# One core of a Trainium2: keys and values of two token blocks turned by VectorE in 32x32 squares and a DRAM round trip in place of TensorE transposes

## The chip, the cores and the metric

The kernel runs on one core of one Trainium2 chip. The metric is the device time of one execution in microseconds (us). Three runs of the kernel before took 2595.07, 2595.23 and 2595.78 us, median 2595.23 us. The profile was taken on one more execution of the same program.

## What is computed

One step of an encoder layer: a wide projection of the normed input, a short convolution (path A), a gated linear attention with a state (path B), three output projections, norms and a gate. All of it is in float32. The change lies in path B, which works on 8 heads of 128 channels in chunks of 64 tokens:

```python
def hgrn2_block(S, q, k, v, logf):
    L = q.shape[1]
    b = jnp.cumsum(logf, axis=1)
    ref = b[:, (L - 1) // 2][:, None]
    qe = q * jnp.exp(b - ref)
    ke = k * jnp.exp(ref - b)
    att = jnp.where(causal, jnp.einsum('bthk,bshk->bhts', qe, ke), 0.0)
    o = jnp.einsum('bhts,bshv->bthv', att, v) + jnp.einsum('bthk,bhkv->bthv', q * jnp.exp(b), S)
    b_last = b[:, -1]
    S_new = jnp.exp(b_last)[..., None] * S + jnp.einsum('bshk,bshv->bhkv', k * jnp.exp(b_last[:, None] - b), v)
    return S_new, o
```

The sum over tokens s in the state update and in `att` times `v` needs keys and values with the tokens on the partitions. The projections give them with the channels on the partitions, so each 128x128 tile of them has to be turned.

## The kernel before

**Blocks.** The 2112 tokens (2048 of a prompt, 64 of a sample) are worked in three blocks of 768, 704 and 640 tokens. Two chunks of 64 tokens make a pair, a full 128x128 tile. A block has 6, 5 and 5 pairs; the second block has the sample's 64 tokens besides. `plan()` puts them into parts: the first four pairs, the other pairs, and the sample alone (called single in the code).

**Products.** Nearly all TensorE time goes into the projections. Two 128-wide output blocks are made together by seven products over half operands (`sgroup`), and each product is 12 matmuls: 4 blocks of the contraction, each as three matmuls of a rounded high part and a rest (lines 444 to 446). The weights' parts come by DMA, which SP asks for: 256 KB each, a raw block and its rest.

**Heads.** For each head `path_b` calls `head_prep`, which runs two such groups: forget gate and query, then output gate and value, 14 products in all. VectorE and ScalarE make the decayed keys `kb` and `ka`, the queries `qe` and `qx`, the values `vt` and the gate `z`. `scaled` (it makes `kb`, lines 993 to 1003, and then `qx`, line 1013) is called after the third product of the second group; `vt` (lines 1022 and 1023) is ready about when that group ends.

**Hooks.** The attention of a head doesn't run at once. `path_b` puts its steps into the list `hooks`, and after each product of the next head `sgroup` takes one entry from it. A step's matmuls are thus queued on TensorE right behind that product (`placed`). In the second and third block a part has four steps (`head_attn`):

- step 0: TensorE transposes of `kb` (line 1068) and `vt` (line 1070), ScalarE copies of both from PSUM to SBUF (lines 1072 and 1073), the products of keys and queries (lines 1083 and 1084) and their masking on VectorE (line 1092);
- step 1: the state updates, one matmul for each pair (line 1098), then a chain of VectorE operations from pair to pair (line 1115);
- step 2: the outputs (lines 1138 and 1140) and their norm, for which POOL computes a power (line 691);
- step 3: the transposes back (line 1156) and the product with the gate (line 1158).

With two or three parts, step 0 of the parts stands behind products 0, 1, 2 of the next head, step 1 behind 3, 4, 5, step 2 behind 6, 7, 8 and step 3 behind 10, 11, 12. At the end POOL stores the head's result to DRAM (line 1166).

**Queues.** Every engine works its own instructions in the compiled order. SP asks for the weights; POOL asks for nearly everything else that moves. A POOL DMA that needs what an earlier one wrote waits in POOL's queue until that one has landed, and all that is behind it on POOL waits too.

**Buffers.** Wide tiles come from one ring of 48. PSUM has 5 banks for products and 3 for the attention.

Of the kernel before, what the change touches and what calls it, by code (L numbers as in the profile page):

```python
# [18 lines left out]
P = 128  # L19
# [74 lines left out]
def hybrid_step(  # L94
# [66 lines left out]
    def ps_attn():  # L161
        return psa.tile([P, 512], F32, tag="pa", name=nm("pa"))
# [773 lines left out]
    def head_prep(bl, hc, hd, first, hs):  # L936
        n, npair = bl["n"], bl["npair"]
        nch, np1 = n // CH, npair * P
        sf, qe = rt(), rt()
        sq = None if first else rt()  # L940

        def sink_f(c, h, x, y):
            if c == 0:
                A.activation(half(sf, h), whole(x, y), AF.Sigmoid)
            else:
                into(half(qe, h), x, y)

        if hs and hd == 0:
            plain_group(FF * 8, QQ * 8, hs, sink_f)
        else:  # L950
            sgroup(FF * 8 + hd, QQ * 8 + hd, hc, sink_f, first)
        if not first:
            A.activation(sq, qe, AF.Sigmoid)
        lg, b, eq = rt(), rt(), rt()
        A.activation(lg, sf, AF.Ln, bias=lb[:, hd : hd + 1], scale=omlb[:, hd : hd + 1])
        if not first:
            V.scalar_tensor_tensor(qe, qe, QK_SCALE, sq, ALU.mult, ALU.mult)
            V.tensor_scalar(sf, sf, nomlb[:, hd : hd + 1], omlb[:, hd : hd + 1], ALU.mult, ALU.add)
        V.tensor_tensor_scan(b, keep[:, :n], lg, 0.0, ALU.mult, ALU.add)
        ref = chunks(b)[:, :, CH // 2 - 1 : CH // 2]  # L960
        V.tensor_tensor(chunks(lg), chunks(b), ref.to_broadcast([P, nch, CH]), ALU.subtract)
        qc = small.tile([P, 2, BN // CH], F32, tag="qc", name=nm("qc"))
        f, r = qc[:, 0, :nch], qc[:, 1, :nch]
        ka, kb, qx, vt, z = hf(npair * CH), rt(), rt(), rt(), rt()

        late = first and hd > 0

        def scaled(after):


            with tc.issue_after(after):
# [12 lines left out]

            ka3 = ka.rearrange("p (g t) -> p g t", t=CH)
            more = npair - 2 * SWAP
            for lo, hi, to in (
                (0, SWAP, ka3[:, more + 1 :: 2, :]),
                (SWAP, 2 * SWAP, ka3[:, more : npair - 1 : 2, :]),
                (2 * SWAP, npair, ka3[:, :more, :]),  # L990
            ):
                own = slice(2 * lo, 2 * hi, 2)
                V.tensor_tensor(to, chunks(sf)[:, own, :], chunks(lg)[:, own, :], ALU.mult)
                scale = f2[:, lo:hi].unsqueeze(2).to_broadcast([P, hi - lo, CH])
                place = slice(2 * lo + (hi <= SWAP), 2 * hi, 2)
                V.tensor_tensor(chunks(kb)[:, place, :], to, scale, ALU.mult)
            for lo, hi in ((0, SWAP), (SWAP, npair)):
                seconds, place = slice(2 * lo + 1, 2 * hi, 2), slice(2 * lo + (hi > SWAP), 2 * hi, 2)
                V.tensor_tensor(chunks(kb)[:, place, :], chunks(sf)[:, seconds, :], chunks(lg)[:, seconds, :], ALU.mult)
            if nch % 2:  # L1000
                end = slice(nch - 1, nch)
                V.tensor_tensor(chunks(kb)[:, end, :], chunks(sf)[:, end, :], chunks(lg)[:, end, :], ALU.mult)
            V.tensor_tensor(f2, f2, f1, ALU.mult)
            if not late:
                queries()

        def queries():
            if first:
                A.activation(qe, qe, AF.Silu)
                V.scalar_tensor_tensor(qe, qe, QK_SCALE, eq, ALU.mult, ALU.mult)  # L1010
            else:
                V.tensor_tensor(qe, qe, eq, ALU.mult)
            V.tensor_tensor(chunks(qx), chunks(qe), f.unsqueeze(2).to_broadcast([P, nch, CH]), ALU.mult)

        def sink_v(c, h, x, y):
            if c == 1:
                n1 = 0
                if h == 0:
                    n1 = 2 * SWAP * CH
                    for odd in range(2):  # L1020
                        c3, to = (slice(o, 2 * SWAP, 2) for o in (odd, 1 - odd))
                        V.tensor_tensor(chunks(vt)[:, to, :], chunks(x[:, :n1])[:, c3, :], chunks(y[:, :n1])[:, c3, :], ALU.add)
                V.tensor_tensor(half(vt, h)[:, n1:], x[:, n1:], y[:, n1:], ALU.add)
# [12 lines left out]
        return dict(eq=eq, f=f, ka=ka, kb=kb, qe=qe, qx=qx, vt=vt, z=z, more=npair - 2 * SWAP, first=first, last=bl["last"], carry=None)  # L1036

    def cols3(t, nt):
        return t[:, : nt * P].rearrange("p (g c) -> p g c", c=P)

    def head_attn(ip, gs, d, hd):

# [19 lines left out]

        p_k, p_v = ps_attn(), ps_attn()
        with placed():
            for i, g in enumerate(gs):
                T.transpose(p_k[:, i * P : i * P + P], cols(d["kb"], g), ident)
            for i, g in enumerate(gs):
                T.transpose(p_v[:, i * P : i * P + P], cols(d["vt"], g), ident)  # L1070
        kt, v = tile3(0), tile3(1)
        A.copy(kt[rows], cols3(p_k, nt)[rows])
        A.copy(v[rows], cols3(p_v, nt)[rows])
        p_a = ps_attn()
        with placed():
            for i, g in enumerate(gs):
# [18 lines left out]
        p_u = ps_attn()  # L1095
        with placed():
            for i in range(nt):
                T.matmul(p_u[:, i * P : i * P + P], kt[:, i, :], v[:, i, :], start=True, stop=True)  # L1098
        ss = tile3()
        prevs = []  # L1100
        sample = gs[0]["sample"]
# [33 lines left out]
        with placed():  # L1135
            for i, g in enumerate(gs):
                dst = p_o[:, i * P : i * P + P]
                T.matmul(dst, att[:, i, :], v[:, i, :], start=True, stop=prevs[i] is None)  # L1138
# [19 lines left out]
        V.scalar_tensor_tensor(z[:, c], p_t[:, P - ln : P - ln + n], g_on[:, hd : hd + 1], z[:, c], ALU.mult, ALU.mult)  # L1158
        yield

    def path_b(bl, hc, first, kept, fills, hs, lead_sums=None):


# [4 lines left out]
        for hd in range(NH):  # L1168
            d = head_prep(bl, hc, hd, first, hs)
            if hd > 0 if first else hd == KH + 1:  # L1170
                next(fills, None)
            assert not hooks
            lead = first and hd == 0
            attn = [head_attn(i, gs, d, hd) for i, gs in enumerate(bl["parts"])]
            hooks.extend([None] * (2 * lead))
            for step in range(4):
# [3 lines left out]
                if lead_sums is not None and not first and step == 2:  # L1180
                    hooks[-1] = partial(next, lead_sums, None)
# [530 lines left out]
```

## Time and profile before

| | |
|---|---|
| three timed runs | 2595.07, 2595.23, 2595.78 us |
| profiled execution, first to last instruction (span) | 2590.9 us |
| TensorE busy (weight loads) | 2572.4 us (2556.1 us) |
| VectorE, ScalarE, POOL busy | 1726.9, 1530.4, 368.3 us |
| granted TensorE clock | 1.000 |
| moved by DMA | 739.87 MB, mean 286 GB/s |

For the profiled execution only the span was recorded. The median of the timed runs is 4.3 us above it: what lies around the span. The heads of the second block run from about 1083 to 1399 us of the span, those of the third from about 1900 to 2180 us.

In a row of the timeline stand the start (us), the busy time (us), the engine, the line, the operation, what is written and read, the shape, and how many were merged (x4). PEld is the load of a matmul's stationary operand. In brackets stands the idle time before it and who ended that.

### The profile page before, as it was taken

Reading aid. Unit: us, or ns where it says so; the run is one execution under the profiler, and the core shown is the slowest. Engines: PE = TensorE matmul, PEld = TensorE weight load, DVE = VectorE, ACT = ScalarE, POOL = GpSimd, SP = SyncE. Lnnn points to the kernel's source line nnn. Section 1 sums busy time; section 2 is a strip of 40 time slices with the busy share of each in tenths; the row PEclk is TensorE's granted clock in tenths of the full one; section 3 lists DMA queues with packets and bytes.
Section 4 is the critical chain, followed back from the end, with each engine's and each line's share of the span. In section 5 each row is a group of like instructions: output and inputs, shape, how many; then the busy total and the mean of one; then the engine's idle time right before and its main releaser. Section 6 shows DMA issues by size and latency. Waiting matters only on the chain.

```text
span 2590.9 us, 47524 instructions
## 1 busy us (share of the span) xinstructions
PE 2572.4 (99%) x16436; PEld 2556.1 (99%) x16436; DVE 1726.9 (67%) x3500; ACT 1530.4 (59%) x2973; POOL 368.3 (14%) x677
## 2 busy tenths in 40 slices
PE   9999999999999999999999999999999999999999
PEld 9999999999999999999999999999999999999998
DVE  7788778888777775466464556987345545336967
ACT  6766676455453764466564555566456665446675
POOL 2011111230022021111111221102100000001011
PEclk9999999999999999999999999999999999999999
DMA  8678777899897888877768998989887788999986
GB/s 325 224 262 288 263 260 273 310 360 308 262 349 238 272 311 269 281 248 233 262 227 287 342 388 313 323 291 334 295 268 251 246 273 264 299 297 323 333 270 200
DMA packets 361234, 739.87 MB, mean 286 GB/s; under 512 B 44119, under 2 KB 48785, under 8 KB 360993
## 3 DMA queue, kind: packets, MB, share of 16 engines
q1 hardware_dynamic: 321696, 582.69, 67.3%
q0 software_dynamic: 39296, 154.14, 16.3%
q8 instruction: 129, 2.11, 0.3%
q14 instruction: 113, 0.92, 0.1%
HBM read 543.44 MB, written 193.22 MB: 284 GB/s over the span
## 4 chain that ended last, share of the span: by engine, by line
PE 90%; DMA 4%; DVE 4%; issue 1%; ACT 1%; SPq 0%; POOL 0%; DVEq 0%; ACTq 0%
PE pg L444 19%; PE pg L446 19%; PE pg L445 19%; PE pg L596 5%; PE pg L595 5%; PE pg L597 5%; PE pg L635 3%; PE pg L634 3%; PE pg L633 3%; PE pa L1098 1%; PE pa L1138 1%; DMA lo<-low 1%; PE pa L1140 1%; PE pa L1084 1%; DMA low<-lo 1%
## 5 line engine op out<-in xcount | busy, mean ns | idle before, releaser
L444 PE MATMUL pg<-r,hi 128*128 128x320 f32 (+2 forms) x3304 | 1086.4, 329 | 1.4 <-DVE r L492 0.7
L445 PE MATMUL pg<-r,hi 128*128 128x320 f32 (+2 forms) x3304 | 1067.6, 323 | 0.0
L446 PE MATMUL pg<-r,lo 128*128 128x384 f32 (+2 forms) x2356 | 768.8, 326 | 5.3 <-DMA lo<-low 3.4
L275 ACT CAST hi<-raw 128x512 fp32r<-128x512 f32 x730 | 449.7, 620 | 515.5 <-PE pg L445 179.2
L444 PEld LDWEIGHTS pg<-r,hi 128*128 128x128 f32 x3304 | 621.5, 188 | 3.3 <-issue 1.0
L445 PEld LDWEIGHTS pg<-r,hi 128*128 128x128 f32 x3304 | 621.9, 188 | 0.0
L446 PEld LDWEIGHTS pg<-r,lo 128*128 128x128 f32 x2356 | 442.5, 188 | 7.9 <-DMA lo<-low 4.4
L446 PE MATMUL pg<-r,s 128*128 128x352 f32 (+1 forms) x948 | 299.4, 316 | 0.3 <-DMA s<-low 0.3
L596 PE MATMUL pg<-r,hi 128*128 128x320 f32 (+2 forms) x864 | 277.4, 322 | 0.6 <-DVE r L228 0.6
L595 PE MATMUL pg<-r,hi 128*128 128x320 f32 (+2 forms) x864 | 275.0, 322 | 0.0
L228 ACT CAST hi<-raw 128x512 fp32r<-128x512 f32 x252 | 155.6, 620 | 155.5 <-PE pg L445 44.0
L228 DVE TENSOR_TENSOR r<-r,r 128x320 fp32r<-128x320 f32 (+7 forms) x354 | 208.7, 608 | 52.9 <-ACT r L228 51.3
L228 ACT CAST r<-r 128x320 fp32r<-128x320 f32 (+7 forms) x354 | 185.9, 557 | 57.0 <-DMA r<-w_blk 13.0
L228 DVE TENSOR_TENSOR lo<-raw,hi 128x512 fp32r<-128x512 f32 x231 | 157.9, 685 | 88.0 <-ACT hi L228 84.2
L597 PE MATMUL pg<-r,lo 128*128 128x352 f32 (+2 forms) x564 | 180.9, 321 | 0.7 <-DMA lo<-low 0.7
L446 PEld LDWEIGHTS pg<-r,s 128*128 128x128 f32 x948 | 177.9, 188 | 0.7 <-DMA s<-low 0.6
L228 ACT CAST hi<-s 128x512 fp32r<-128x512 f32 x156 | 96.2, 618 | 120.1 <-PE pg L445 102.0
L634 PE MATMUL pg<-r,hi 128*128 128x384 f32 (+2 forms) x512 | 166.8, 326 | 0.2 <-DVE r L228 0.2
L633 PE MATMUL pg<-r,hi 128*128 128x384 f32 (+2 forms) x512 | 166.3, 328 | 0.2 <-ACT hi L275 0.2
L596 PEld LDWEIGHTS pg<-r,hi 128*128 128x128 f32 x864 | 162.2, 188 | 2.4 <-DVE r L228 1.7
L595 PEld LDWEIGHTS pg<-r,hi 128*128 128x128 f32 x864 | 161.3, 188 | 1.3 <-ACT r L228 0.6
L458 ACT COPY hf<-pg 128x352 f32<-128x352 f32 (+2 forms) x354 | 157.1, 446 | 1.7 <-PE pg L446 1.3
(403 smaller groups left out, 4114.3 us busy)
## 6 DMA issues: line engine op xcount, KB each, us to landing
raw<-w_blk SPq DMA_DIRECT2D x577, 256.0 KB, 4.1
raw<-S SPq DMA_DIRECT2D x444, 256.0 KB, 4.2
lo<-low SPq DMA_DIRECT2D x422, 256.0 KB, 4.1
s<-low SPq DMA_DIRECT2D x308, 256.0 KB, 4.0
low<-lo SPq DMA_DIRECT2D x271, 256.0 KB, 3.8
S<-s SPq DMA_DIRECT2D x152, 256.0 KB, 3.6
low<-r POOLq DMA_DIRECT2D x54, 256.0 KB, 5.1
r<-w_blk POOLq DMA_DIRECT2D x52, 256.0 KB, 6.9
```

The lines of the kernel that those rows point to most:

```text
L228: return A.copy(hi, src).ins, V.tensor_tensor(lo, src, hi.bitcast(F32), ALU.subtract).ins
L275: A.copy(hi, raw)
L444: add(hi[:, k, :], xhi, start=start and k == 0, stop=False)
L445: add(hi[:, k, :], xlo, start=False, stop=False)
L446: last[0] = add(lo[:, k, :], xhi, start=False, stop=k == KH - 1).ins
L458: copied = A.copy(got[n], ps[bank])
L595: add(hi[:, k, :], xhi, start=start and k == 0, stop=False)
L596: add(hi[:, k, :], xlo, start=False, stop=False)
L597: last[0] = add(lo[:, k, :], xhi, start=False, stop=k == KH - 1).ins
L633: T.matmul(ps, hi[:, k % 4, :], xhi[:, c], start=k == ks[0], stop=False)
L634: T.matmul(ps, hi[:, k % 4, :], xlo[:, c], start=False, stop=False)
L635: last[0] = T.matmul(ps, lo[:, k % 4, :], xhi[:, c], start=False, stop=k == ks[-1]).ins
```

## The change

Only the second and third block are touched (`first` is false), and there only the pairs; the sample's single part keeps its TensorE transposes.

- `turned` is new. For `kb` at the end of `scaled`, and for `vt` after the second group, one VectorE instruction transposes all 32x32 squares of the 5 pairs at once: a square holds 32 channels, and every fourth token of a pair. It reads with a step of 4 elements. The result goes into a tile that is no longer needed (`b` for keys, `sf` for values), keys with a step of 5 elements between channels, and POOL stores it to DRAM as 128 rows of 640 elements.
- `in_rows` is new. After both stores POOL loads the two tiles back with tokens on the partitions: 128x4 runs of 160 elements for each.
- In `head_attn` the transposes, their PSUM tiles and the ScalarE copies fall away for pairs. Keys are read by the state update with a step of 5 elements, values in four runs of 32.
- The hooks are written out anew: both pair parts update the state behind product 6 instead of 3 and 4, and make their outputs behind product 8 instead of 6 and 7. The single part goes ahead of them.

```diff
+            if not first:
+                turned("tk", kb, b, npair)
...
+        by_token = None
+        if not first:
+            turned("tv", vt, sf, npair)
+            by_token = [in_rows(kind, npair) for kind in ("tk", "tv")]
...
+    def turned(kind, src, out, npair):
+        n = npair * P
+        blocks4 = out[:, :n].rearrange("p (j a g) -> p g j a" if kind == "tk" else "p (j g a) -> p g j a", j=4, a=32)
+        V.transpose(blocks4, src[:, :n].rearrange("p (g b j) -> p g j b", b=32, j=4))
+        turning[kind] = dram.tile([P, n], F32, tag=f"{kind}{npair}", name=nm(kind), bufs=2)
+        G.dma_start(turning[kind], out[:, :n])
+
+    def in_rows(kind, npair):
+        t = rt(npair * P)
+        G.dma_start(t.rearrange("q (i c) -> q i c", i=4), turning[kind].rearrange("(i b) (j c) -> (b j) i c", i=4, j=4))
+        return t.rearrange("q (k g) -> q g k", g=npair) if kind == "tk" else t.rearrange("q (i g a) -> q g i a", i=4, a=32)
...
+        if d["by_token"] is not None and not single:
+            kt, v = (t[:, o0 // P : o0 // P + nt] for t in d["by_token"])
+        else:
...
-                T.matmul(p_u[:, i * P : i * P + P], kt[:, i, :], v[:, i, :], start=True, stop=True)
+                T.matmul(p_u[:, i * P : i * P + P], kt[:, i], v[:, i], start=True, stop=True)
...
+            if not first:
+                pairs, one = attn[:2], attn[2:]
+                piece = lead_sums and [partial(next, lead_sums, None)]
+                for steps in (
+                    pairs[:1], pairs[1:], one, None, None, one, pairs, one, pairs, piece, one, pairs[:1], pairs[1:],
+                ):
+                    hooks.append(partial(each, [s if callable(s) else partial(next, s) for s in steps]) if steps else None)
```

How this changes the compiled order is shown at two places, both in a head of the third block. Names are those of the program with a number for each buffer; in the changed kernel lines have moved: 1056 is the VectorE transpose, 1058 the store and 1063 the load of a turned tile, 1198 the store of a head's result (1166 before), 1015 makes `qx` (1013), 1024 and 1025 the values (1022, 1023), 1186 is the product with the gate (1158). In brackets stand the engines and DMA queues that the instruction waits for.

POOL before, from the store of one head's result (`o`) to the end of the next head's norm:

```order
L1166 DMA o_24562<-r_23979 128x640 [waits DVE_49]
L1129 DMA hgrn_p<-state_24746 128x128 [waits DMASW4_49,DVE_49]
L691 TENSOR_TENSOR ms_24789<-ms_24789,mhalf 128x4 [waits DVE_49,Pool_49]
L691 TENSOR_TENSOR ms_24871<-ms_24871,mhalf 128x1 [waits DVE_49,Pool_49]
```

POOL in the changed kernel, the same stretch of a head (`tk` keys and `tv` values in DRAM):

```order
L1058 DMA tk_23986<-r_23843 128x640 [waits DMASW5_49,DVE_49]
L1198 DMA o_24058<-r_23489 128x640 [waits DMASW6_49,DVE_49]
L1063 DMA r_24063<-tk_23986 128x4x160 [waits DMASW7_49,DMASW5_49,PE_49]
L1058 DMA tv_24061<-r_23664 128x640 [waits DVE_49,Activation_49]
L1063 DMA r_24065<-tv_24061 128x4x160 [waits DMASW1_49,DMASW0_49]
L1157 DMA hgrn_p<-state_24241 128x128 [waits DVE_49]
L691 TENSOR_TENSOR ms_24341<-ms_24341,mhalf 128x4 [waits DVE_49]
L691 TENSOR_TENSOR ms_24351<-ms_24351,mhalf 128x1 [waits DVE_49]
```

Four DMAs have come in, in one line: the store of the keys, their load, which waits for that store, the store of the values behind it, and their load, which waits for that store.

VectorE before, from the last operation of `scaled` to the end of the second group (the values are the rows of lines 1022 and 1023):

```order
L1003 TENSOR_TENSOR qc_24389<-qc_24389 128x5
L464 TENSOR_TENSOR hf_24450<-hf_24450,pg_24508 128x320
L1013 TENSOR_TENSOR r_24392<-r_24166,qc_24389 128x640
L1158 TENSOR_SCALAR r_23979<-pa_24522,vec,r_23979 128x512
L1158 TENSOR_SCALAR r_23979<-pa_24542,vec,r_23979 128x128
L1022 TENSOR_TENSOR r_24393<-hf_24450,pg_24462 128x2x64
L1029 TENSOR_TENSOR r_24394<-pg_24437,r_24394 128x320
L1022 TENSOR_TENSOR r_24393<-hf_24450,pg_24462 128x2x64
L1023 TENSOR_TENSOR r_24393<-hf_24450,pg_24462 128x64
L1023 TENSOR_TENSOR r_24393<-hf_24450,hf_24475 128x320
L485 TENSOR_TENSOR hf_24576<-hf_24450,pg_24477 128x320
```

VectorE in the changed kernel, the same stretch:

```order
L1003 TENSOR_TENSOR qc_24656<-qc_24656 128x5
L464 TENSOR_TENSOR hf_24717<-hf_24717,pg_24794 128x320
L1015 TENSOR_TENSOR r_24659<-r_24471,qc_24656 128x640
L1056 STREAM_TRANSPOSE r_24649<-r_24658 128x5x128
L1186 TENSOR_SCALAR r_24258<-pa_24822,vec,r_24258 128x512
L1031 TENSOR_TENSOR r_24661<-pg_24704,r_24661 128x320
L1024 TENSOR_TENSOR r_24660<-hf_24717,pg_24719 128x2x64 x2
L1025 TENSOR_TENSOR r_24660<-hf_24717,pg_24719 128x64
L1025 TENSOR_TENSOR r_24660<-hf_24717,hf_24732 128x320
L1186 TENSOR_SCALAR r_24258<-pa_24845,vec,r_24258 128x128
L485 TENSOR_TENSOR hf_24860<-hf_24717,pg_24760 128x320
L1056 STREAM_TRANSPOSE r_24470<-r_24660 128x5x4x32
```

The transpose of the keys stands behind lines 464 and 1015, ahead of the values; that of the values stands behind line 485. In seven of the eight heads of the third block the keys' transpose stands there; in its first head, and in every head of the second block, it comes directly behind line 1003.

More of the change, by code (lines that the diff above doesn't have):

```diff
@@ L1061, in cols @@
             return t[:, end - P : end]
[L1065 to L1073, printed above, removed]
+        if d["by_token"] is not None and not single:
+            kt, v = (t[:, o0 // P : o0 // P + nt] for t in d["by_token"])
+        else:
+            p_k, p_v = ps_attn(), ps_attn()
+            with placed():
+                for i, g in enumerate(gs):
+                    T.transpose(p_k[:, i * P : i * P + P], cols(d["kb"], g), ident)
+                for i, g in enumerate(gs):
+                    T.transpose(p_v[:, i * P : i * P + P], cols(d["vt"], g), ident)
+            kt, v = tile3(0), tile3(1)
+            A.copy(kt[rows], cols3(p_k, nt)[rows])
+            A.copy(v[rows], cols3(p_v, nt)[rows])
         p_a = ps_attn()
@@ L1159, in head_attn, with each @@
         yield
+    def each(steps):
+        for step in steps:
+            step()
     def path_b(bl, hc, first, kept, fills, hs, lead_sums=None):
@@ L1175, in path_b @@
             hooks.extend([None] * (2 * lead))
[L1176 removed]
+            if not first:
[5 more added lines that the diff above has]
+                    hooks.append(partial(each, [s if callable(s) else partial(next, s) for s in steps]) if steps else None)
+            for step in range(4 * first):
                 hooks.extend(partial(next, g) for g in attn)
                 hooks.extend([None] * (0 if step == 3 else 3 - len(attn) - (lead and step == 0) + (step == 2)))
[L1180 to L1181 removed]
             hooks.append(partial(keep_z, hd, d["z"]))
```

8 lines of the change are left out of this document (6 added, 2 removed).

## The prediction

> **What bounds the kernel now.** I read the page first, then the waits of TensorE, then the table by stages. The page's first part and its row of the granted clock:
>
> ```profile
> PE 2572.4 (99%) x16436; PEld 2556.1 (99%) x16436; DVE 1726.9 (67%) x3500; ACT 1530.4 (59%) x2973; POOL 368.3 (14%) x677
> ...
> PEclk9999999999999999999999999999999999999999
> ```
>
> TensorE is busy for all but 18.5 us of 2590.9 at full clock. The waits of TensorE, longest first (total, times, longest), and the stages (length, then busy PE, PEld, DVE, ACT, POOL, the clock, the DMA engines' share, GB/s): a head of the second block, path A behind it, a head of the third block.
>
> ```profile
> PE pg L446 <- DMA lo<-low: 3.4, 2, 2.6
> ...
> 1153.00:1188.00 35.00, 35.00 (x242) 34.88 (x241) 21.60 (x59) 22.66 (x43) 4.90 (x8) 1.00 0.73 239
> ...
> 1399.00:1600.00 201.00, 200.18 (x1240) 199.61 (x1239) 112.84 (x219) 112.50 (x231) 42.98 (x95) 1.00 0.96 339
> ...
> 2008.00:2041.00 33.00, 33.00 (x242) 32.96 (x242) 19.04 (x52) 22.28 (x41) 3.28 (x5) 1.00 0.77 246
> ```
>
> In the heads TensorE never stands still. So whatever leaves its queue there is gained in full, and whatever it is made to wait for is lost in full. Nothing else counts.
>
> **What it removes.** The transposes of keys and values, all blocks together, and the first steps of one head in the second block on TensorE (start, busy of the merged group):
>
> ```profile
> L1070 PE MATMUL pa<-ident,r 128*128 128x128 f32 x136 | 24.0, 273 | 0.0
> L1068 PE MATMUL pa<-ident,r 128*128 128x128 f32 x136 | 23.9, 272 | 0.0
> ```
>
> ```profile
> 1162.09 0.60 PE L1068 MATMUL pa<-ident,r 128*128 128x128 f32 x4
> 1162.52 0.60 PE L1070 MATMUL pa<-ident,r 128*128 128x128 f32 x4
> 1162.96 0.39 PE L1083 MATMUL pa<-r,hf 128*128 128x128 f32 x2
> ...
> 1166.24 0.27 PE L1068 MATMUL pa<-ident,r 128*128 128x128 f32 x1
> 1166.35 0.27 PE L1070 MATMUL pa<-ident,r 128*128 128x128 f32 x1
> ...
> 1171.21 1.05 PE L1098 MATMUL pa<-r,r 128*128 128x128 f32 x8
> 1174.03 0.38 PE L1098 MATMUL pa<-one,one 128*128 128x128 f32 x2
> ```
>
> The 272 ns of one are latency; what one costs is its distance to the next. Eight start between 1162.09 and 1162.96, so 0.109 us each; the lone ones at 1166.24 and 1166.35 agree. Of the 272, the first block keeps 6 pairs x 8 heads x 2 = 96 and the sample 16. The other 160 go: **160 x 0.109 = 17.4 us gained**, 1.09 us in each of 16 heads. The ScalarE copies of them go too:
>
> ```profile
> L1073 ACT COPY r<-pa 128x512 f32<-128x512 f32 x24 | 14.4, 599 | 0.0
> L1072 ACT COPY r<-pa 128x512 f32<-128x512 f32 x24 | 14.1, 587 | 0.0
> ```
>
> That frees 1.2 us of ScalarE in a head of some 22 busy us. TensorE waits for nothing there, so I count it as nothing.
>
> **What it adds: a chain from the keys to the state update.** VectorE transposes the keys; POOL stores them; POOL's load of the keys waits until that store has landed; the store of the values is queued behind that load, and the load of the values waits for this store. Only when it has landed can TensorE begin the state updates behind product 6. I follow it through a head of the third block. VectorE and TensorE there:
>
> ```profile
> 2001.44 0.69 DVE L1149 TENSOR_REDUCE ms<-r 128x4 f32<-128x512 f32 x1 [1.93 <-ACT r L1148]
> 2002.07 0.82 DVE L957 SCALAR_TENSOR_TENSOR r<-r,r 128x640 f32<-128x640 f32 x1
> ...
> 2004.19 0.69 DVE L1151 TENSOR_TENSOR r<-pa,ms 128x512 f32<-128x512 f32 x1 [1.22 <-POOL ms L691]
> ...
> 2005.32 1.48 DVE L959 TENSOR_TENSOR_SCAN r<-keep,r 128x640 f32<-128x640 f32 x1
> ...
> 2012.40 0.82 DVE L1013 TENSOR_TENSOR r<-r,qc 128x640 f32<-128x640 f32 x1
> ...
> 2014.98 0.48 DVE L1023 TENSOR_TENSOR r<-hf,hf 128x320 f32<-128x320 f32 x1
> ```
>
> ```profile
> 2015.72 0.60 PE L1068 MATMUL pa<-ident,r 128*128 128x128 f32 x4
> ...
> 2023.89 1.05 PE L1098 MATMUL pa<-r,r 128*128 128x128 f32 x8
> 2026.54 0.38 PE L1098 MATMUL pa<-one,one 128*128 128x128 f32 x2
> ```
>
> And the DMAs of such tiles that POOL asks for (KB, median us to landing), then the spread of landings of line 1166 (stores of a head's result) and of line 1249 (loads):
>
> ```profile
> o<-r POOLq DMA_DIRECT2D x8, 352.0 KB, 5.1
> ...
> o<-r POOLq DMA_DIRECT2D x8, 320.0 KB, 5.6
> r<-o POOLq DMA_DIRECT2D x8, 320.0 KB, 6.1
> ```
>
> ```profile
> DMA to landing us min/median/max: 2.8/5.0/6.2
> ```
>
> ```profile
> DMA to landing us min/median/max: 3.8/6.0/10.3
> ```
>
> *When TensorE wants it.* Before, the state update starts 8.17 us behind the head's first step (2015.72 to 2023.89). Now 1.09 us of transposes are gone and three products more lie between. A product takes 1.75 us (2023.89 and 0.9 for the eight starts, to 2026.54). So 2015.72 + 8.17 - 1.09 + 5.25 = **2028.05**.
>
> *When it comes.* The order shown above puts the keys' transpose behind line 1013, which ends at 2013.22. No row shows a VectorE transpose. It handles 640 elements a lane, as do the rows at 0.82 (line 957) and 1.48 (the scan); I take 0.82, an operation with one pass, and keep 1.48. So the keys' store goes out at 2014.04 and lands 5.6 later, 2019.64. POOL issues their load (0.54) and at 2020.18 the store of the values: these are done at 2015.46 (line 1023), some 1.5 us later with the two transposes and line 485 in the queue, and so wait only for POOL. It lands at 2025.78, and their load, 6.1 later, at **2031.9: 3.8 us too late**. In seven heads that is 26.9; in the block's first head the transpose comes before lines 464 and 1013, some 1.1 us sooner: 2.7. Together 29.6 us.
>
> In the second block the products are longer. The state update before is 9.12 us behind the first step (1162.09 to 1171.21), a product takes 1.93, and the sample's own update (0.2) goes ahead: 1162.09 + 9.12 - 1.09 + 5.79 + 0.2 = 1176.1. The keys of the next head, and POOL's rows that give the period of a head:
>
> ```profile
> 1192.86 0.22 DVE L1002 TENSOR_TENSOR r<-r,r 128x64 f32<-128x64 f32 x1
> ```
>
> ```profile
> 1144.52 0.54 POOL L1125 DMA_DIRECT2D hgrn_s<-state  x1 [18.22 <-DVE state L1123]
> ...
> 1179.57 0.54 POOL L1125 DMA_DIRECT2D hgrn_s<-state  x1 [16.12 <-DVE state L1123]
> ```
>
> The keys' transpose follows line 1003 at 1193.15 and ends at 1193.97; one period of 35.05 earlier that is 1158.92. Its store lands 5.1 later, two issues follow (keys' load, result's store, 1.08), and the values' store goes out at 1165.1, lands at 1170.2, and is loaded by 1176.3: 0.2 late, in eight heads 1.6 us.
>
> **The sum:** -17.4 + 29.6 + 1.6 = +13.8 us on the profiled 2590.9; carried to the median of the three runs, 2595.2, this is **2609 us**.
>
> **What else it adds.** *Loads in 512 runs.* All these DMAs move 128 rows; the loads of turned tiles move 512 runs of 640 bytes. The nearest rows are POOL's issues of 5 rows and of 128:
>
> ```profile
> L766 POOL DMA_DIRECT2D xrs<-r x2: 528/528/528, 619.8 to 1494.3; - x2
> ```
>
> ```profile
> L775 POOL DMA_DIRECT2D r<-xrs x2: 538/543/548, 765.3 to 1647.8; - x2
> ```
>
> 123 more rows cost 15 ns, so I take no more than 0.54. The other bound is four issues' time, 1.6 us more for each of two loads, in up to 16 heads 51 us. *Keys with a step.* The state update's stationary operand now has a step of 20 bytes; loads without one take this:
>
> ```profile
> L1098 PEld LDWEIGHTS pa<-r,r x224: 187/192/192, 105.3 to 2162.8; 128*128 128x128 f32 x112
> ```
>
> They hide behind the matmul before. If the load with a step took one start distance longer (1.05 us for eight, less latency, so 0.112), 160 of them would cost 17.9 us; I take nothing. *VectorE* gets 2 x 0.82 us in a head of which it works 19 to 22 of 33 to 35; the evictions behind it have had no wait to show. *The DMA engines* get 4 x 0.33 MB a head, about 40 GB/s on 240. At share 0.96 path A lost 0.8 us of 201; over 540 us of heads that would be 2 us. *Later steps.* Outputs to transposes back had four products and have three, 5.2 us; the norm took 3.4 us (2001.44 to the end of line 1151) and 0.6 on ScalarE. Covered, by 1 us. Behind the values' load POOL holds the state's store and that norm's power, both needed later.
>
> **Rivals.** *The round trip fits.* If the DMAs land as fast as the fastest rows (2.8, 2.8 and 3.8), the values are back at 2024.0, 4 us ahead, and the whole gain stays: 2595.2 - 17.4 = 2578. Against it: the median is twice that, and the keys' load runs beside the values' store. By the Trainium skill's "DMA: Bandwidth & Descriptors", section "Anatomy of one DMA — SWDGE (gpsimd) path", a POOL DMA takes 2.0 us plus bytes / 436 GB/s, here an estimate of 2.75 us, which is this rival; the medians above, taken beside the weights' traffic, are twice it.
>
> *The keys' step counts.* With the waits as forecast it adds up to 17.9 us: 2627. With no waits it eats the gain: 2596, no change. It decides once a load no longer hides behind a matmul. The Trainium skill's "SBUF — State Buffer", section "Door 1: The DMA port swizzle (why `[64,N]` ≈ `[32,N]`)", says that every access on a new 16-byte line pays a penalty, as a step of 20 bytes would; no run here shows it.
>
> *A half-hidden trip.* With landings 1 us shorter each, the third block waits 0.8 us and the second none: 2583; with 0.5 us shorter, 2.3 us: 2595.
>
> **How the numbers follow.** Forecast, waits that outweigh the gain: 0.48, 2601 to 2630. The same with the step of the keys: 0.12, up to 2645. The trip fits: 0.24, 2576 to 2583. Half hidden: 0.16, of it 0.05 below 2590 and 0.11 within 0.2% (5 us, about what a measurement of this kernel can tell from no change). So faster 0.29, same 0.11, slower 0.60. The range must hold both ends, 2577 to 2636: it leaves out the fastest few and the worst of the step of keys and of the 512 runs. The forecast's own range is 2601 to 2630.
>
> **What would show it.** Right: TensorE idle before the state update of pairs, ended by the DMA of the values, some 3 to 4 us in each head of the third block and near nothing in the second; POOL idle before the loads, ended by the stores. Wrong: no such wait; stores of turned tiles landing in 3 us; a VectorE transpose of 1.5 us or more; weight loads at the state update well over 192 ns.

## The result, and the profile after

Six timed runs of the changed kernel gave a median of 2674.45 us (2658.51 to 2682.29), six of the kernel before beside them 2595.15 us (2590.57 to 2596.14). The ratio is 1.0311, 95% interval 1.0288 to 1.0334: **slower by 79 us**, above the forecast of 2609 and outside its range. The profiled execution has a span of 2669.8 us, 78.9 more than before. Its time of 2671.51 us is 1.7 us above its span, and so it is in the runs below; of the 4.3 us between the span and the median of the kernel before, some 2.6 were thus a difference between executions and not what lies around the span.

The page of the changed kernel, its first part and the granted clock in 40 slices:

```profile
PE 2588.6 (97%) x16276; PEld 2571.6 (96%) x16276; DVE 1763.0 (66%) x3532; ACT 1512.4 (57%) x2909; POOL 408.0 (15%) x741
...
PEclk9999999999999999999999999999998898999999
```

TensorE has 160 instructions fewer and is busy 16 us longer, and for the first time the clock dips, in the third block. The waits of TensorE (total, times, longest) in the second block, which are the stretch 1080 to 1400 us, and in the third, 1900 to 2260 us:

```profile
PE pa L1126 <- DMA r<-tv: 18.1, 7, 4.5
...
PE pa L1126 <- DMA r<-tv: 47.3, 7, 7.4
```

Line 1126 is the state update. Its only large releaser is the load of the turned values, 65.4 us in 14 of 16 heads; in the kernel before no row of waits came to more than 3.4 us. The two heads that did not wait begin 52 and 54 us after the head before them in their block, the others 31 to 41: there the keys' store was issued 13 and 16 us ahead of the head's first step, in the head shown below 0.8. POOL stands in front of that load because the values' store has not landed:

```profile
POOL r L1063 <- DMA tv<-r: 79.1, 12, 8.3
```

**One head of the third block, the counterpart of the one in the prediction.** First TensorE, whose first step of the head starts at 2063.38, then VectorE, then POOL (start, busy, engine, line, idle before and its releaser):

```profile
2063.38 0.38 PE L1111 MATMUL pa<-r,hf 128*128 128x128 f32 x2
...
2083.02 2.55 PE L1126 MATMUL pa<-r,r 128*128 128x128 f32 x10 [7.14 <-DMA r<-tv]
```

```profile
2060.79 1.47 DVE L1056 STREAM_TRANSPOSE r<-r 128x640 f32<-128x640 f32 x1
...
2064.64 1.37 DVE L1056 STREAM_TRANSPOSE r<-r 128x640 f32<-128x640 f32 x1
```

```profile
2062.56 0.60 POOL L1058 DMA_DIRECT2D tk<-r  x1 [7.25 <-DVE r L1056]
2064.66 0.54 POOL L1198 DMA_DIRECT2D o<-r  x1 [1.49 <-DVE r L1186]
2069.53 0.77 POOL L1063 DMA_DIRECT2D r<-tk  x1 [4.33 <-PE pg L446]
2070.30 0.54 POOL L1058 DMA_DIRECT2D tv<-r  x1
2077.21 0.76 POOL L1063 DMA_DIRECT2D r<-tv  x1 [6.37 <-DMA tv<-r]
```

The reader sees the whole chain: the values are turned by 2066.0, but their store stands behind the keys' load until 2070.30; it needs 6.9 us until POOL can go on, and the load 5.8 more. TensorE was ready at 2083.02 - 7.14 = 2075.88.

**Two costs beside the wait.** The weight loads of the state update with their step of 20 bytes (ns min/median/max), and the starts behind a wait against those of the one third-block head that did not wait, at 2167:

```profile
L1126 PEld LDWEIGHTS pa<-r,r x80: 294/316/321, 1963.2 to 2246.7; 128*128 128x128 f32 x80
```

```profile
2167.05 2.34 PE L1126 MATMUL pa<-r,r 128*128 128x128 f32 x10
...
2172.75 0.38 PE L1166 MATMUL pa<-r,att 128*128 128x128 f32 x2
```

```profile
2089.18 0.38 PE L1166 MATMUL pa<-r,att 128*128 128x128 f32 x2
```

```profile
2206.03 2.56 PE L1126 MATMUL pa<-r,r 128*128 128x128 f32 x10 [7.45 <-DMA r<-tv]
...
2213.68 0.38 PE L1166 MATMUL pa<-r,att 128*128 128x128 f32 x2
```

A load takes 316 ns where it took 192. From the state update to the products with the states it is 5.70 us without a wait before it (2167.05 to 2172.75), 6.16 behind the wait of the head shown (2083.02 to 2089.18) and 7.65 behind another (2206.03 to 2213.68). The stages of the head shown say why (length, busy PE, PEld, DVE, ACT, POOL, granted clock, DMA share, GB/s): the wait, the state update, the next two products.

```profile
2076.00:2083.00 7.00, 0.00 (x0) 0.01 (x1) 0.40 (x1) 3.73 (x5) 0.76 (x1) 0.73 0.79 294
2083.00:2085.60 2.60, 2.58 (x11) 2.60 (x12) 0.40 (x2) 0.00 (x0) 0.00 (x0) 0.50 0.00 0
2085.60:2089.20 3.60, 3.60 (x25) 3.60 (x25) 3.42 (x8) 0.94 (x2) 0.54 (x1) 0.94 0.18 19
```

After seven idle microseconds TensorE starts at half its clock and gets it back some 3 us later. Of the seven waiting heads of the third block this one lost the least: the seven took 6.16 to 7.65 us for this stretch, 8.9 us more in all than without a wait, and the full clock came back 3 to 6 us after the start. In the second block the seven waits cost 7.0 us by the same count (6.48 us without a wait). Together that is **16 us**. e3 below, which does the same work with nearly no wait, bears out both bases (5.71 and 6.47 to 6.49 us in its heads that do not wait) and has TensorE busy for 14.9 us less (2573.7).

The Trainium skill, "TensorE: Matmul & The Clock Gate", section "Part 1: The HAM clock gate (the "warmup" mystery)", states half rate after an idle window of about 3.4 us and full rate after as long a busy one. The trace agrees with the half rate (0.50) and roughly with the way back, but not with the length of the idle time: waits of 1.53, 1.60 and 1.67 us in the second block were followed by 0.50 too, and only one of 0.83 us was not.

**The sum of the loss**, against the 78.9 us of span: transposes gone -17.4 (160 x 0.109); waits +65.4; weight loads with a step +15 (e5 below); clock +16. That is 79, and nothing is left for the work beside the path, which cost 10.1 us where nothing waited for the trip (e2 below). A delay of TensorE ahead of a wait only shortens the wait, which would hide it; that was not separated, and the terms come from different runs, so the sum may be off by some microseconds.

### The profile page after: what moved, and what is told of

The parts are those of the page before. It is cut to its first block, busy times and chain, and to the rows that moved or that the text cites. A ratio compares the mean times of both kernels' runs of the same rounds, so it can differ in the third digit from the quotient of the medians.

```text
span 2669.8 us, 47393 instructions
## 1 busy us (share of the span) xinstructions
PE 2588.6 (97%) x16276; PEld 2571.6 (96%) x16276; DVE 1763.0 (66%) x3532; ACT 1512.4 (57%) x2909; POOL 408.0 (15%) x741
```

## The experiments

Theory after the result: the round trip is late in nearly every head, its latency is most of the loss, and the step of the keys and the clock are the rest. Rivals: the new hook list, or the added work on VectorE and DMA, costs by itself. The first four kernels take the change apart; they ran beside a kernel before of 2590.06 us (2585.38 to 2594.32).

**e1_hooks: the new order alone.** `turned` and `in_rows` are not called, so TensorE transposes as before.

```diff
-                turned("tk", kb, b, npair)
...
-            turned("tv", vt, sf, npair)
-            by_token = [in_rows(kind, npair) for kind in ("tk", "tv")]
```

> Only the new list of hooks: pairs update their states behind product 6 and make their outputs behind product 8; transposes stay on TensorE, nothing goes through DRAM. Theory (the loss is the wait for the turned values, the slower load of keys with a step and the clock that falls in the wait, less 17.4 us of transposes): nothing of that is here, so 2595 us within 4 us. Rival (the later steps themselves cost, because state chain and norm have one product less): up to 1 us in each of 16 heads, about 2611 us, with TensorE idle before outputs or before the transposes back.

Measured 2590.05 us, ratio 1.0002 (0.9993 to 1.0011). State updates two or three products later, and outputs one or two later, cost nothing.

**e2_unused: the round trip made, not used.**

```diff
-        if d["by_token"] is not None and not single:
+        if False:
```

> The changed kernel with the round trip made in full (VectorE transposes, stores, loads) but not used: keys and values are transposed on TensorE as before. Theory: TensorE waits for none of it, so 2595 to 2601 us. Rival (the side work itself costs: 21 MB more on the DMA engines, 44 us more on VectorE, a POOL queue that stands): above 2610 us, with TensorE waiting for weights or for evictions.

Measured 2600.12 us, ratio 1.0045 (1.0031 to 1.0059): 10.1 us more, above the theory's guess of up to 6 and far under the rival. In its trace TensorE waits once for a masking on VectorE, which now works 1765 us; the rest of the 10 is spread and was not pinned to one engine:

```profile
PE pa L1096 <- DVE att L1120: 4.7, 1, 4.7
```

**e3_stale: the same loads, of tiles that landed a head ago.**

```diff
+        landed[kind] = turning.get(kind)
-        turning[kind] = dram.tile([P, n], F32, tag=f"{kind}{npair}", name=nm(kind), bufs=2)
+        turning[kind] = dram.tile([P, n], F32, tag=f"{kind}{npair}", name=nm(kind), bufs=3)
...
-turning[kind].rearrange("(i b) (j c) -> (b j) i c", i=4, j=4)
+(landed[kind] or turning[kind]).rearrange("(i b) (j c) -> (b j) i c", i=4, j=4)
```

> The changed kernel, but each head from the second of a block on loads the turned tiles of the head before, which landed long ago; the first head of the whole kernel's second block loads its own. Left out: the right keys and values in the state update and the outputs, so it is not the reference's result. Same work, no wait for the trip. Theory: the waits (65 us) and the falls of the clock (some 9 us) go, the slow key loads (19 us) stay, the transposes (17.4 us) stay away: 2595 to 2602 us, weight loads at the state update still 314 ns. Rival (the round trip costs by its traffic, not by its latency): above 2620 us.

Measured 2594.45 us, ratio 1.0025 (1.0014 to 1.0035). This is 4.4 us above the kernel before beside it, where the changed kernel was 79.3 above its own: the same DMAs, the same VectorE work and the same weight loads with a step, but with no store of the same head to wait for, take 75 us less. The loss is latency, with the clock that falls in it, and not load. Transposes gone and weights with a step come to -2.3 us (-17.4 and +15.1), so 6.7 us are left for the work beside the path and for the one wait for the values that remains. The clock is back at 0.998:

```profile
PE pa L1127 <- DMA r<-tv: 2.0, 1, 2.0
```

**e5_step: the kernel before with the step alone.** ScalarE writes the keys into a tile with a step of 5 elements; all else is as before.

```diff
         kt, v = tile3(0), tile3(1)
+        if not d["first"] and not single:
+            kt = rt(5 * P).rearrange("q (k g) -> q g k", g=5)[:, :nt]
```

> The kernel before with one thing changed: ScalarE writes the transposed keys of pairs of the second and third block with a step of 5 elements between channels, so the state update loads its weights with that step. Theory: 160 weight loads at about 0.23 us from start to start instead of 0.11, 1.2 us in each of 16 heads: 2614 us, weight loads 314 ns against 189. Rival (the 314 ns are due to the cold clock or the DMA traffic, and a step costs nothing): 2595 us and 189 ns.

Measured 2605.21 us, ratio 1.0062 (1.0049 to 1.0075): 15.1 us more with no new wait, 0.095 us for each of 160 loads. Weight loads that take 192 ns hide behind the matmul before; these do not. The row below holds 96 loads of the first block without a step too; the others have a median of 315 ns:

```profile
L1100 PEld LDWEIGHTS pa<-r,r x224: 187/309/320, 104.5 to 2173.7; 128*128 128x128 f32 x112
```

The next four change the place of the wait; the kernel before beside them took 2589.83 us (2588.15 to 2592.96).

**e6_order: the values' store ahead of the keys' load on POOL.**

```diff
-        G.dma_start(turning[kind], out[:, :n])
+        stored[kind] = G.dma_start(turning[kind], out[:, :n]).ins
...
-            by_token = [in_rows(kind, npair) for kind in ("tk", "tv")]
+            with tc.issue_after(stored["tv"]):
+                by_token = [in_rows(kind, npair) for kind in ("tk", "tv")]
```

> The changed kernel with the values' store ahead of the keys' load in GpSimd's queue (both loads are put behind the values' store); nothing else differs. Theory (the wait is the values' round trip, and part of it is its store queued behind the keys' load): in the third block's head at 2063 us the values were turned by 2066.0 and their store was issued at 2070.3, so the store, the load and TensorE's start all come about 4.3 us earlier there, and the wait before the state update falls from 7.1 to about 3 us; in the second block, where the store was issued within 0 to 3 us of being ready, a part of 18 us goes. Waits for the values from 65 to about 30 us, some of the clock's loss with them, 2632 us in all. Rival (the queue is no part of it: a store issued earlier lands no earlier, because the DMA engines are busy with the weights then): the wait stays over 6 us a head in the third block and the time over 2660 us.

Measured 2626.10 us, ratio 1.0134 (1.0117 to 1.0151): 36 us above the kernel before beside it in place of 79, so 43 us better than the changed kernel from two instructions exchanged in one queue, as the theory had it. The waits fell from 65.4 us to

```profile
PE pa L1127 <- DMA r<-tv: 27.8, 10, 4.4
```

and the values' stores also land sooner, now that no load of 320 KB goes ahead of them (whether that is the reason was not tested by itself; median us to landing, the changed kernel first, then this one):

```profile
tv<-r POOLq DMA_DIRECT2D x16, 320.0 KB, 6.7
```

```profile
tv<-r POOLq DMA_DIRECT2D x16, 320.0 KB, 5.4
```

**e7_late: state updates two products later.** The new list, with the outputs behind 9 and 10 and the transposes back behind 13:

```diff
-                    pairs[:1], pairs[1:], one, None, None, one, pairs, one, pairs, piece, one, pairs[:1], pairs[1:],
+                    pairs[:1], pairs[1:], one, None, None, None, None, one, pairs, one, pairs, piece, one, pairs + [partial(keep_z, hd, d["z"])],
```

> The changed kernel with the pairs' state updates two products later still (behind product 8 instead of 6), the products with the states behind 9 and 10, the transposes back and the spill of the head's output behind 13; queue and keys as in the changed kernel. Theory (the round trip is a latency of its own, the same whenever TensorE asks): each wait falls by the two products, some 4 us: third block from 7.1 to about 3 a head, second block near none; 65 to about 25 us of waits, less of the clock's loss, 2628 us in all. Rival (the loads wait for tiles that the state updates themselves free, so that a later update makes later loads): the waits fall by less than 2 us a head and the time stays over 2650 us.

Measured 2637.16 us, ratio 1.0183 (1.0168 to 1.0198). The waits for the values are gone but for one, more than the theory's 4 us a head, and others have come that neither theory named, before the transposes back (line 1184):

```profile
PE pa L1184 <- DVE lone L1179: 13.5, 7, 2.0
PE pa L1184 <- DVE ms L688: 11.4, 7, 1.6
PE pa L1184 <- DVE one L1179: 4.5, 12, 0.4
...
PE pa L1126 <- DMA r<-tv: 2.5, 1, 2.5
```

**e8_both: order, two products later, and the keys copied by ScalarE** behind product 7 into the tile from which they were stored, so that the weights have no step.

```diff
-            kt, v = (t[:, o0 // P : o0 // P + nt] for t in d["by_token"])
+            kt, v = cols3(d["b"][:, o0:], nt), d["by_token"][1][:, o0 // P : o0 // P + nt]
...
+                flat = [partial(A.copy, cols3(d["b"], npair), d["by_token"][0])]
```

> The changed kernel with both of these (values' store ahead of the keys' load, state updates two products later) and the keys copied by ScalarE, five chunks in one instruction behind product 7, from the loaded tile with its step of 20 bytes into the tile from which they were stored, so that the state update reads weights without a step. Theory: 4.3 and some 4 us against waits of 7 leave next to none (under 10 us in all), the weights cost 189 ns again, and what is left is 17.4 us of removed transposes against 4 to 10 us of side work: 2577 to 2590 us, best guess 2583. Rival (the copy on ScalarE or the longer life of the ring's tiles holds up the weight products): over 2595 us.

Measured 2627.46 us, ratio 1.0144 (1.0129 to 1.0159): the theory missed by 44 us. No wait for the values is left, but the waits before the transposes back are those of e7:

```profile
PE pa L1185 <- DVE lone L1180: 13.4, 7, 1.9
PE pa L1185 <- DVE ms L688: 11.1, 7, 1.6
PE pa L1185 <- DVE one L1180: 3.4, 9, 0.4
PE pg L444 <- ACT hf L458: 2.9, 1, 2.9
PE pg L444 <- ACT hi L275: 2.8, 2, 2.1
```

That is 27.9 us; the rival's ScalarE shows with 5.7 only. The clock, 0.992 over the run, takes a part of the rest; how much was not measured.

**e9_keys: only the keys go through DRAM**, the values by TensorE and ScalarE as before.

```diff
-            turned("tv", vt, sf, npair)
-            by_token = [in_rows(kind, npair) for kind in ("tk", "tv")]
+            by_token = [in_rows("tk", npair)]
```

> The changed kernel with only the keys turned and sent through DRAM, and the values of pairs turned by TensorE and copied by ScalarE as in the kernel before. Theory (it is the values' trip that is late; the keys' store leaves 13.3 us before the state update and would land at about its start): waits for the keys under 1 us a head; 2590 less 8.7 us (80 transposes) plus 16 us (weights with a step) plus about 4 us of side work: 2601 us. Rival (any trip at this distance is late, the keys' too): 2 us a head or more, 2625 us or more.

Measured 2611.37 us (2607.04 to 2618.74), ratio 1.0087 (1.0068 to 1.0105). No row of TensorE's waits names the keys' load, so the keys alone are in time, as the theory had it. The time is 10 us above the theory's; those 10 are not explained.

Two kernels then put the parts together (kernel before beside them 2590.33 us, 2585.95 to 2596.28).

**e10_copy: the order, and the keys copied by GpSimd** behind the issue of both loads.

```diff
+                G.tensor_copy(cols3(b, npair), by_token[0][:, :npair])
```

> The changed kernel with the values' store ahead of the keys' load, as in the run before with that change alone, and a copy by GpSimd, behind the issue of the values' load, of the loaded keys into the tile from which they were stored; the state update reads weights without a step. Products in the places of the changed kernel. Theory (the step of 20 bytes costs 120 ns for each of 160 weight loads): 16 to 19 us less than with the order alone, 2608 us, weight loads at 189 ns and the waits for the values unchanged at about 28 us. Rival (the step costs only beside other effects, or the copy comes too late and TensorE waits for GpSimd): within 8 us of 2626 us.

Measured 2617.36 us (2613.82 to 2621.26), 27 us above the kernel before where e6 was 36 above: 9 us gained, just more than the rival's 8 and well under the theory's 16 to 19. Busy TensorE fell by 16.2 us from the one profile to the other (2582.2 to 2566.0), but the profile of e6 is of its slowest run and that of e10 of its fastest, so the price of the step is better taken from e5. The weight loads are back at 192 ns and the waits are as in e6:

```profile
L1128 PEld LDWEIGHTS pa<-r,r x256: 186/192/338, 105.1 to 2188.8; 128*128 128x128 f32 x128
```

```profile
PE pa L1128 <- DMA r<-tv: 29.2, 12, 4.0
```

**e11_fit: e10 with the pairs one product later**, the single parts where they are.

```diff
-                    pairs[:1], pairs[1:], one, None, None, one, pairs, one, pairs, piece, one, pairs[:1], pairs[1:],
+                    pairs[:1], pairs[1:], one, None, None, one, None, one + pairs, piece, pairs, one, None, pairs,
```

> As the kernel with order and copy, with the pairs' state updates one product later (behind 7), their products with the states behind 9 instead of 8, and their transposes back behind 12; the single chunks stay where they are in the changed kernel. Theory: 28 us of waits for the values fall by two us a head to about 8; the norm of the pairs' outputs now lies behind VectorE's key work, as with two products, where the transposes back waited 28 us, but one product earlier: some 5 to 12 us of waits there; 2590 to 2600 us, best guess 2594, no better than the kernel before. Rival (the waits before the transposes back come from the single chunks' norms, which stay early here): none of them, 2582 to 2588 us, faster than before.

Measured 2627.02 us, ratio 1.0144 (1.0123 to 1.0166). Both missed. The waits before the transposes back are as large one product later as two:

```profile
PE pa L1186 <- DVE ms L688: 29.5, 14, 2.6
PE pa L1168 <- DVE lone L1181: 6.3, 7, 1.0
...
PE pa L1128 <- DMA r<-tv: 1.6, 1, 1.6
```

The kind was as the theory had it: below are VectorE's rows in a head of the third block, the last of whose products with the states starts at 2057.69. The norm's sum (line 1179) stands behind all key work of the next head (lines 1014 to 1015) and behind the keys' turn:

```profile
2059.00 0.82 DVE L1014 TENSOR_TENSOR r<-r,r 128x640 f32<-128x640 f32 x1
...
2061.75 0.81 DVE L1015 TENSOR_TENSOR r<-r,qc 128x640 f32<-128x640 f32 x1
2062.49 1.41 DVE L1058 STREAM_TRANSPOSE r<-r 128x640 f32<-128x640 f32 x1
2063.74 0.63 DVE L1179 TENSOR_REDUCE ms<-r 128x4 f32<-128x512 f32 x1
```

It is a step, not a slope: the key work enters the program after the third product of the second group. An output behind product 8 has its norm ahead of that, one behind 9 or 10 has it behind.

**e12_ahead: e11 with the norm ahead of the key work.** The entry of the third product is called before `scaled`, and the key work is queued behind the norm's sum.

```diff
                 if n == 2 and mid is not None:
+                    if not first:
+                        hook()
                     mid(copied.ins)
...
+            with behind_all(() if first else normed):
...
-            V.tensor_reduce(ms[rows, :nt], on[rows], axis=mybir.AxisListType.X, op=ALU.add)
+            normed[:] = [V.tensor_reduce(ms[rows, :nt], on[rows], axis=mybir.AxisListType.X, op=ALU.add).ins]
```

> The kernel before this one (order, copy, state updates behind product 7, their products with the states behind 9) with VectorE's queue changed: the sums of the pairs' norms, and what follows of the norm, stand ahead of the next head's key work instead of behind its transpose in squares; nothing else differs. Theory (the 30 us before the transposes back are the norm queued behind some 5.5 us of key work and 1.4 us of the keys' turn): these waits go, the keys leave 2 to 4 us later, which the products between cover: 2588 to 2598 us, best guess 2592. Rival (the key work itself is then late, and TensorE waits for the keys at the state update or for the products of the next head instead): waits of 1 us or more a head under another name, over 2608 us.

Measured 2597.68 us (2591.26 to 2604.43) against 2591.95, ratio 1.0025 (1.0013 to 1.0037): 6 us above the kernel before where e11 was 37 above, so 31 us from the order of the same instructions. The sum now stands ahead of the key work and the wait before the transposes back is gone:

```profile
2071.50 0.68 DVE L1183 TENSOR_REDUCE ms<-r 128x4 f32<-128x512 f32 x1
...
2072.51 0.82 DVE L1018 TENSOR_TENSOR r<-r,r 128x640 f32<-128x640 f32 x1
...
2077.81 1.51 DVE L1062 STREAM_TRANSPOSE r<-r 128x640 f32<-128x640 f32 x1
```

```profile
PE pa L1132 <- DMA r<-tv: 10.6, 6, 2.1
PE pa L1172 <- DVE lone L1185: 6.4, 7, 1.0
```

**e13_tight: e12 with the pairs' state updates behind product 8, their outputs still behind 9, the single parts' outputs behind 6** (and their transposes back behind 11 instead of 10).

```diff
-                    pairs[:1], pairs[1:], one, None, None, one, None, one + pairs, piece, pairs, one, None, pairs,
+                    pairs[:1], pairs[1:], one, None, None, one, one, None, pairs, pairs, piece, one, pairs,
```

> The kernel before this one (order, copy, norm ahead of the key work) with the pairs' state updates behind product 8 instead of 7 and their products with the states still behind 9, and the single chunks' products with the states behind 6 instead of 7, so that their bank is free before the pairs'. Theory (two waits are left, 10.6 us for the values in six heads and 6.4 us for the single chunks' bank, and both go; the states, five steps of some 0.35 us on VectorE, are made beside the one product between): 2580 to 2590 us, best guess 2584, faster than the kernel before. Rival (one product is too short for VectorE to make the states, which stand there beside its scan of 1.5 us): TensorE waits 1 to 2 us a head for the states, 16 to 30 us, and the time is over 2594 us.

Measured 2579.10 us (2576.32 to 2582.58) against 2593.31 (2587.91 to 2597.39), ratio 0.9953 (0.9940 to 0.9967): **faster than both kernels**, 14 us (0.5%) below the one before, which the changed one exceeded by 79. The span is 2574.6; the wait for the values is next to nothing:

```profile
PE pa L1132 <- DMA r<-tv: 1.9, 2, 1.2
```

## Why the prediction was wrong

- **The gain.** 17.4 us from 160 transposes was not measured by itself. e13, with nearly no wait, has TensorE busy for 2555.0 us, 17.4 less than the kernel before (15.9 less than e1, which has all the transposes too), is idle as long (19.6 us for 18.5), and keeps 14.2 us of time with the work beside the path still in it.
- **When TensorE wants the values** was right: 12.33 us behind the head's first step, measured 12.50 (2063.38 to 2075.88). In the second block 14.0, measured 14.2 in the head shown below (1332.69 to 1351.10 less 4.20). That this order costs nothing was right too (e1).
- **When they come is the step that failed.** The prediction had them 16.2 us behind the first step of the head ("at 2031.9: 3.8 us too late"); they came at 19.6 in the head shown. The mechanism stood as written, the keys' load in front of the values' store included, and e3 and e6 show it; its terms were too small, all but the last one: VectorE's transpose 1.47 us for 0.82; 0.3 us from its end to the store's issue, which was left out; the keys' store 6.1 us and 0.9 more to the next issue for 5.6; the load's issue 0.77 for 0.54; the values' store 6.6 and 0.3 for 5.6; the last load 5.8 for 6.1. Each was taken at a median or at a one-pass row, with nothing between them; together the chain was 3.4 us short, and 7.1 us of wait is nearly twice 3.8. The row of the keys' load names a reader of the tile that it overwrites, but that can have added some 0.3 us at most: in both blocks 30 of the 32 loads are issued 0.3 to 0.6 us behind the landing of their store, this one 0.9, and only one, at 1991.14, 3.0.
- **The second block** was to wait 0.2 us a head and waited 2.6 in seven. It was put at the edge, so that every error of the chain became a wait. In one of its heads (TensorE, then POOL) the values' store alone took 8.3 us from its issue to the next, where 5.1 was taken. Both blocks: 65.4 us for 31.2, so 34.2 of the 65.1 us by which the forecast was short (78.9 for 13.8).

```profile
1332.69 0.38 PE L1111 MATMUL pa<-r,hf 128*128 128x128 f32 x2
...
1351.10 2.55 PE L1126 MATMUL pa<-r,r 128*128 128x128 f32 x10 [4.20 <-DMA r<-tv]
```

```profile
1336.62 0.55 POOL L1058 DMA_DIRECT2D tv<-r  x1
1344.91 0.76 POOL L1063 DMA_DIRECT2D r<-tv  x1 [7.75 <-DMA tv<-r]
```

- **The keys with a step** were taken at nothing, with 17.9 us as the bound. They cost 15.1 us alone (e5). The bound was right and the choice was wrong: the 192 ns of a plain load was known to hide, and no row said that a longer one would. The rule of the Trainium skill, "SBUF — State Buffer", section "Door 1: The DMA port swizzle (why `[64,N]` ≈ `[32,N]`)", that an access on each new 16-byte line pays, agrees with 316 against 192 ns; no other step was measured, so that the line is the cause is not shown.
- **The clock** was left out of every case, though the forecast itself had TensorE idle for 3.8 us in seven heads: 16 us that the waits cost behind themselves. With the waits and the step this makes up the miss (34.2, 15.1 and 16).
- **Loads in 512 runs** cost 0.23 us of issue each and no longer landing (6.0 and 6.1 for 6.1): near the low end, as taken.
- **The work beside the path** on VectorE, POOL and the DMA engines stood in no term of the sum; the DMA engines alone were put at up to 2 us. It cost 10.1 us in e2 and, less the one wait of 2.0, 4.7 in e3.
- **The rivals.** "The round trip fits" and "half hidden" took landings below the medians; the medians of both blocks came to 5.1 and 6.7 us for the stores, 6.1 and 6.0 for the loads. The 2.75 us that the Trainium skill's "DMA: Bandwidth & Descriptors", section "Anatomy of one DMA — SWDGE (gpsimd) path", would give is little more than half of the smallest of these, beside the weights' traffic; the measurement decides. "The keys' step counts" came true on top of the forecast, and its 2627 was 47 us short of the result: 34 of waits and 16 of clock, less 3 by which the step stayed under its bound.

## What to carry to other kernels

A chain through memory is the sum of its hops, and each hop has three parts: landing, the gap to the next issue, and the issue; where a lateness of some microseconds decides, take the slow side of each, and ask what is queued ahead of the last store. Price a wait of TensorE with the clock that it loses behind it. A step that is moved later to cover a latency moves its successors past other work in another engine's queue: there the cost can come all at once, as with the norm behind the key work. Look at the queue on both sides of the new place before the size of the gain.

## What the hardware showed that was not expected

- A weight load of 128x128 float32 with a step of 20 bytes takes about 315 ns (median) for 192 without, and 8 or 10 of them in a row are no longer hidden: 0.095 us each (e5).
- TensorE's granted clock fell to 0.50 behind each of 13 waits of 1.5 to 7.5 us, and not behind one of 0.83 us. Each such fall cost 0.5 to 2.0 us behind the wait.
- VectorE's transpose in 32x32 squares takes 1.32 to 1.47 us for 128x640 float32 in the changed kernel, read with a step of 16 bytes, where a one-pass operation takes 0.82; what of it is the step was not separated.

```profile
L1056 DVE STREAM_TRANSPOSE r<-r 128x640 f32<-128x640 f32 x32 | 44.4, 1388 | 0.0
```

- POOL's issue of a DMA of 512 runs takes 0.77 us, of 128 rows 0.54 to 0.60.
- A GpSimd copy of 128x640 float32 with a step took 1.38 us on average (e10); TensorE's weight loads waited for it once, 3.4 us.
